# Retrieval layer of an encoder block: six more first-product blocks made ahead, a fourth buffer for finished blocks, and splits that follow the block in front

## The chip, the core and the metric

One core of a Trainium2 chip. The metric is the device time of one execution in microseconds (us). Engines are called PE (matrix products), PEld (its weight loads), DVE (vector), ACT (scalar activations), POOL (GpSimd) and SP (the engine whose queue issues most plain DMAs). In the trace a queue's own entries carry a q (ACTq, SPq).

## The reference, cut to what matters

The program is one whole encoder layer on 1,024 tokens of width 1,024. The change touches only its last part, a retrieval feed-forward layer with 16,384 experts. For every token eight heads choose 16 experts each:

```
s1 = q[..., :half] . keys[0];  s2 = q[..., half:] . keys[1]
top16 of s1, top16 of s2, top16 of their sums  -> expert ids e, scores
g = softmax(scores)
h = gelu(x . peer_u[e])          # first product, 128 numbers per token
x = x + sum_k g*h * peer_v[e]    # second product
```

## The kernel before, in words

The 1,024 tokens are eight tiles of 128. Three tiles (`NG`) are served by **gathers**: for each of 128 choices POOL fetches one row of `peer_u` per token with an indirect DMA (L1154), DVE takes the dot product with the token (L1187), and later the same happens with `peer_v`, where DVE adds the scaled row to an accumulator (L1199). That is 768 fetches, each of 128 rows of 4 KB, and 768 DVE operations.

The other five tiles, 640 tokens, are served **densely**. The experts are 128 blocks of 128. For every block i the first product is h_i = gelu(U_i . x): 48 matmuls of 320 columns, written as four groups of 12 (two token halves, two halves of the contraction). The gates, scattered into a dense array `GD` in DRAM, multiply h_i (L1479, `amake1`), the result is cast to a high part `ah` (ACT, L1481) and a low part `al` (DVE, L1487), and the second product adds it to 640 x 1,024 outputs.

Each weight block is split into a high and a low part. For U_i that is `usplit`: a cast `uh` and a subtraction `ul`; the subtraction runs on POOL (L119), and the cast on POOL in the first of the two phases below and on ACT in the second. For V_i it is `vsplit`: `vh` on ACT, `vl` on POOL.

**The first phase** begins at about 780 us. It makes the gates and, beside them, the first products of some blocks ahead. The order is written by a loop in which each turn has one group of four tokens of gate work (PE `pg` L1100 and three small products L1082 to L1085, ACT copies L1110, every eighth turn a store of `GD`, L1113) and one step of 12 matmuls of a first product (`ustep`, L1236). `K0` = 33 blocks spread over the 128 are made ahead, 31 (`KM`) in this loop and the last two in the passage that follows. Their results go to DRAM (`HDm`). With every turn a credit of planned microseconds is given to a list of DVE and POOL work: the top-16 searches of tiles, and gather steps priced at `GCOST` = 3.0. A turn with a block step gives 3.05, one without gives 2.6. The gather steps of this phase take the dot product with the token in SBUF (`QB`, parts 0 and 1) and write its unused products to part 2 of `QB`.

**The main loop** (L1600 to L1628) has 127 turns. In each the second product of block i goes to four accumulators that stay in PSUM (`accum`, 12 matmuls of 512 columns) and to three of six outputs that take turns in one PSUM bank `prot` (`rotate`, 6 matmuls each); DVE adds the bank to X (L1561) before the next `rotate` may start. Between them stand three places (`ugroup`) where one group of 12 matmuls (L1496) of a first product not made ahead is issued: 95 blocks, 380 groups, 381 places. The gather steps that are left are dealt evenly over the turns. A finished block waits in one of three buffers of 128 x 640 (`hfree`): two of their own and one in parts 0 and 1 of `QB`. Blocks made ahead are loaded back into these buffers (`hload`, L1473). At the head of a turn POOL receives the subtraction of V_{i+1} and, in three turns of four, right behind it the subtraction of the next U (`uahead`).

All queues run in order; PSUM bank `hps` of the first products is single.

Of the kernel before, what the change touches and what calls it, by code (L numbers as in the profile page):

```python
# [10 lines left out]
BF = mybir.dt.bfloat16  # L11
# [3 lines left out]
ALU = mybir.AluOpType  # L15
# [16 lines left out]
NK = 128  # L32
# [7 lines left out]
TB = 32  # L40
GCH = 4
NPERS = 4
K0 = 33
WIN = 2
NVI = 3
NO2 = 2
GPE = 1.4
GCOST = 3.0
KT = 2
GLAST = 1  # L50
FD = 2
# [20 lines left out]
def peer_block(tc, I, out):  # L72
    nc = tc.nc
    ctx = ExitStack()
    V, A, G, PE, SY = nc.vector, nc.scalar, nc.gpsimd, nc.tensor, nc.sync
# [51 lines left out]
    with ExitStack() as fr:  # L127
# [55 lines left out]
        with ExitStack() as st:  # L183
            a_ = st.enter_context(tc.tile_pool(name="A", bufs=1))
            ps = st.enter_context(tc.tile_pool(name="psA", bufs=2, space=PSUM))
# [184 lines left out]
            for j, nm in enumerate(["q_norm_g", "k_norm_g"]):  # L370
                a = I[nm]
# [120 lines left out]
        with ExitStack() as st:  # L492
            b_ = st.enter_context(tc.tile_pool(name="B", bufs=1))
            ps = st.enter_context(tc.tile_pool(name="psB", bufs=1, space=PSUM))
# [270 lines left out]
            for u in range(NU + 4):  # L765
                g = (u + 4) // 4
# [23 lines left out]
                for ch in ORD:  # L790
                    r = parts(ch)
# [33 lines left out]
    TD = ND * P  # L825
    KM = K0 - KT
# [290 lines left out]
    class Gather:  # L1117
# [51 lines left out]
        def adv(self, n=1):  # L1169
            for _ in range(n):  # L1170
                if not self.ready():
                    return
                self.fill()
                ph, t, k = self.seq[self.nc]
                r = self.rows.pop(self.nc)
                self.nc += 1
                ps = self.ps
                if ph == 0:
                    h = self.h(t) if ps is None else ps
                    if k == 0:  # L1180
                        self.hh[t] = gp.tile([P, P], F32, name=f"hh{t}")
                        if ps is not None:
                            self.stage(t)
                            A.copy(ps, self.staged[t])
                            self.slots.append(self.staged.pop(t))
                    jk = QB[:, 2, :].bitcast(BF)
                    V.scalar_tensor_tensor(jk, r, 1.0, h, op0=ALU.mult, op1=ALU.mult,  # L1187
                                           accum_out=self.hh[t][:, k:k + 1])
                else:
                    if k == 0:  # L1190
                        aa = gp.tile([P, P], F32, name=f"aa{t}")
                        A.activation(aa[:], self.hh[t][:], AF.Gelu_apprx_tanh)
                        V.tensor_tensor(aa[:], aa[:], gg[t][:], op=ALU.mult)
                        self.aa[t] = aa
                    xt = X[:, t, :]
                    if k == 0 and ps is not None:
                        A.copy(ps, xt)
                    to = xt if ps is None else ps
                    V.scalar_tensor_tensor(to, r, self.aa[t][:, k:k + 1], to, op0=ALU.mult, op1=ALU.add)  # L1199
                    if k == P - 1 and ps is not None:  # L1200
                        A.copy(xt, ps)
                self.slots.append(r)
                if ph and k == P - 4 and t + 1 < NG and ps is not None:
                    self.stage(t + 1)
# [36 lines left out]
    def gelu_(hps, pool, bufs):  # L1241
        ho = pool.tile([P, TD], F32, name="ho", tag="ho", bufs=bufs)
        A.activation(ho[:].rearrange("p (a b) -> p a b", a=len(segs)), hps[:, :len(segs), :SW], AF.Gelu_apprx_tanh)  # L1243
        return ho
# [40 lines left out]
    def k_gat():  # L1285
        if not ks.get("gat") or not gat.ready():
            return None
        gat.adv(1)
        return GCOST

    def kstep():
        order = [("gen", k_gen), ("topk1", k_topk1), ("gat", k_gat)]
# [49 lines left out]

    ust = dict(i=0, seg=0, hps=None, prev=None)

    def ustep():
        i = ust["i"]
        if i >= KM:
            return 0.0
        if i == 0 and ust["seg"] == 0:
            uload(US[0])  # L1350
            uload(US[1])
            usplit(US[0])
        sg = ust["seg"]
        if sg == 0:
            ust["hps"] = hbank([P, 2, 512], "hps")
        useg(US[i], ust["hps"], 2 * sg, 2 * sg + 2)
        if sg == 1 and ust["prev"] is not None:
            ho = gelu_(ust["prev"], up, 1)
            SY.dma_start(HDm[i - 1], ho[:])
        if sg == 1 and i < KM:  # L1360
            usplit(US[i + 1])
            if i + 2 < K0:
                uload(US[i + 2])
        ust["seg"] += 1
        if ust["seg"] == 4:
            ust["seg"] = 0
            ust["i"] += 1
            ust["prev"] = ust["hps"]
        return 1.65
# [34 lines left out]
    while True:  # L1404
# [4 lines left out]
            break  # L1409
        dt = max(dt + GPE * did, KB)  # L1410
        kadv(dt, dt)
    ho = gelu_(ust["prev"], up, 1)
    SY.dma_start(HDm[KM - 1], ho[:])
    while ks["n2"] < len(korder):
        clk["t"] += 2.0
        kstep()
# [2 lines left out]
    with ExitStack() as vs:  # L1419
# [45 lines left out]
            CH[i] = (vh, vl)  # L1465

        hfree = [vp.tile([P, TD], F32, name=f"ho{j}")[:] for j in range(2)]
        hfree.append(QB[:, 0:2, :].rearrange("p a b -> p (a b)")[:, :TD])

        def hload(i):  # L1470
            if i in UI and i not in HO and i < NK:
# [41 lines left out]


        ulist = [i for i in range(NK) if i not in UI]
        ug = dict(g=0, split=0, load=0, ps=None)

        def uahead():
            m = ug["g"] // 4
            if ug["split"] < min(m + 2, len(ulist)):  # L1520
                usplit(ulist[ug["split"]])
                ug["split"] += 1
                if ug["load"] < len(ulist):
                    uload(ulist[ug["load"]])
                    ug["load"] += 1

        def ugroup():
            m, q = divmod(ug["g"], 4)
            if m >= len(ulist):
                return  # L1530
            i, (hf, d) = ulist[m], divmod(q, 2)
            if ug["split"] <= m:
                uahead()
            if d == 0:
                ug["ps"] = ubank()
            uhalf(i, hf, ug["ps"], d * DC // 2, (d + 1) * DC // 2)
            if d == 1:
                if hf == 0:
                    HO[i] = hfree.pop(0)
                ugelu(HO[i], hf, ug["ps"])  # L1540
            ug["g"] += 1

        def uready(i):
            while i not in UI and ulist.index(i) >= ug["g"] // 4:
# [55 lines left out]
        for i in range(NK - 1):  # L1600
            nx = i + 1
            ng = gat0 + -(-(ngat - gat0) * min(nx, nb) // nb) - gat.nc
            gs = [0] * 3
            for j in range(ng):
                gs[SPOTS[j % len(SPOTS)]] += 1
            hload(nx)
            if len(hfree) > 1:
                hload(i + 2)
            loads(i + 2)
            vsplit(nx)  # L1610
            uahead()
            rs_ = [w for w in range(len(rot)) if i % WIN == w % WIN]
            rotate(rs_[0], i, False)
            accum(i, (0,))
            ugroup()
            gat.adv(gs[0])
            rotate(rs_[1], i, False)
            accum(i, (1,))
            ugroup()
            uready(nx)  # L1620
            amake1(nx)
            gat.adv(gs[1])
            amake2(nx)
            rotate(rs_[2], i, False)
            accum(i, (2, 3))
            ugroup()
            gat.adv(gs[2])
            CH.pop(i - WIN, None)  # L1628
        accum(NK - 1, range(len(pers)))
# [71 lines left out]
```

## Time and profile before

| | |
|---|---|
| median of 3 runs | 2993.06 us (2991.23 to 2999.02) |
| the profiled execution | 2996.14 us, of which the span of instructions is 2994.4 us |
| granted PE clock over the span | 0.979 |
| PE busy | 2799.0 us (93%) |
| DVE busy | 2463.6 us (82%) |
| POOL busy | 1953.6 us (65%) |
| DMA | 710.33 MB, mean 237 GB/s |

Shares of busy time are means over stages that differ. A stage's row gives busy microseconds and number of instructions in the order PE, PEld, DVE, ACT, POOL, then the granted PE clock, the busy share of the DMA engines and GB/s. A line of the timeline gives start, duration, engine, line, operation, output and inputs, and how many were merged; in square brackets stand the idle time just before it and what ended that. Matmuls are pipelined: a matmul's duration is longer than the distance to the next, and the distances between starts tell the pace.

### The profile page before, as it was taken

To read this page: it belongs to the slowest core of one execution; us is meant where nothing else is said; L and a number is where in the kernel's file an instruction comes from. 1 tells how busy PE (TensorE), PEld (TensorE's weight loads), DVE (VectorE), ACT (ScalarE), POOL (GpSimd) and SP (SyncE) were. 2 spreads that over 40 slices of the span, in tenths; PEclk is the share of its full clock that TensorE was granted. 3 is DMA by queue.
4 is the path that set the end of the run, shared out by engine and by line. 5 is a ranking of instruction groups with operands and counts; after the bars stand their busy time and mean duration, and the time that the engine had idled before them with its cause. 6 is when DMAs were issued, how large, how long until landed. Compare 5 with 4: busy or idle time off the path is not lost.

```text
span 2994.4 us, 44528 instructions
## 1 busy us (share of the span) xinstructions
PE 2799.0 (93%) x16042; PEld 2475.3 (83%) x16048; DVE 2463.6 (82%) x4465; ACT 1149.2 (38%) x2376; POOL 1953.6 (65%) x1558
## 2 busy tenths in 40 slices
PE   7878899899989899978999999999999999999997
PEld 6767778698978788867888888888888888888886
DVE  5889988468666967864899988988899999999998
ACT  3216566342577577663222222222222222222222
POOL 2578842104445766764777777777777777777775
PEclk9989999999999999999999999999999999999999
DMA  4111000044334667676899898999999998989996
GB/s 131 46 68 36 8 1 15 33 159 129 106 142 149 219 228 266 211 276 251 330 336 345 332 337 330 349 334 353 335 348 335 349 347 333 341 333 337 341 342 228
DMA packets 296719, 710.33 MB, mean 237 GB/s; under 512 B 25264, under 2 KB 135216, under 8 KB 296368
## 3 DMA queue, kind: packets, MB, share of 16 engines
q0 software_dynamic: 110592, 402.70, 35.2%
q1 hardware_dynamic: 156800, 252.85, 25.1%
q10 hardware_dynamic: 29104, 51.91, 4.6%
q8 instruction: 126, 2.06, 0.3%
q14 instruction: 97, 0.79, 0.1%
HBM read 640.46 MB, written 66.91 MB: 236 GB/s over the span
## 4 chain that ended last, share of the span: by engine, by line
PE 55%; DVE 20%; DMA 8%; issue 7%; POOL 4%; ACT 4%; ACTq 1%; SPq 0%; another core or an unknown queue 0%; POOLq 0%; DVEq 0%
PE hps L1496 15%; PE hps L1236 5%; PE prot L122 5%; PE prot L123 4%; PE prot L124 4%; DVE y L146 3%; PE pg L1100 3%; PE acc L122 3%; PE acc L124 3%; PE acc L123 3%; DMA rows<-peer_v,ei 2%; DMA rows<-peer_u,ei 2%; DVE ga L1199 2%; DVE ho L1479 2%; DVE PT L119 2%
## 5 line engine op out<-in xcount | busy, mean ns | idle before, releaser
L1496 PE MATMUL hps<-HN,uh 128*128 128x320 f32 x3072 | 683.9, 310 | 8.1 <-ACT ho L1243 5.3
L1496 PEld LDWEIGHTS hps<-HN,uh 128*128 128x128 f32 x3072 | 530.4, 189 | 42.4 <-issue 5.5
L1496 PE MATMUL hps<-HN,ul 128*128 128x320 f32 x1536 | 475.6, 310 | 0.0
L1199 DVE SCALAR_TENSOR_TENSOR ga<-rows,aa,ga 128x1024 f32<-128x1024 f32 x330 | 424.0, 1285 | 27.5 <-DMA rows<-peer_v,ei 18.1
L1154 POOL DMA_INDIRECT rows<-peer_u,ei x339 | 360.1, 1062 | 108.0 <-issue 68.7
L119 POOL TENSOR_TENSOR vl<-vr,vh 128x1024 fp32r<-128x1024 f32 x128 | 308.8, 2413 | 156.9 <-ACT vh L116 108.5
L1154 POOL DMA_INDIRECT rows<-peer_v,ei x330 | 326.9, 991 | 112.6 <-issue 72.5
L1187 DVE SCALAR_TENSOR_TENSOR QB<-rows,ga 128x1024 bf16<-128x1024 f32 x271 | 329.7, 1216 | 31.3 <-DMA rows<-peer_u,ei 25.1
L122 PE MATMUL prot<-vh,ah 128*128 128x512 f32 x762 | 309.0, 406 | 27.9 <-DVE X L1561 18.6
L119 POOL TENSOR_TENSOR ul<-ur,uh 128x1024 fp32r<-128x1024 f32 x127 | 324.5, 2555 | 2.6
L1561 DVE TENSOR_TENSOR X<-X,prot 128x512 f32<-128x512 f32 x384 | 262.1, 682 | 65.5 <-PE prot L124 55.2
L123 PE MATMUL prot<-vl,ah 128*128 128x512 f32 x762 | 301.1, 395 | 0.4 <-POOL vl L119 0.4
L124 PE MATMUL prot<-vh,al 128*128 128x512 f32 x762 | 297.5, 390 | 0.0
L1496 PEld LDWEIGHTS hps<-HN,ul 128*128 128x128 f32 x1536 | 289.5, 188 | 0.0
L1506 ACT ACTIVATE ho<-hps 128x320 f32<-128x320 f32 x128 | 55.8, 436 | 493.3 <-PE hps L1496 456.2
L1110 ACT COPY gblk<-pg 128x128 f32<-128x128 f32 x640 | 175.6, 440 | 99.2 <-PE pg L1100 74.2
L116 ACT CAST vh<-vr 128x1024 fp32r<-128x1024 f32 x128 | 133.7, 1045 | 203.3 <-DMA vr<-peer_v 196.0
L1236 PE MATMUL hps<-HN,uh 128*128 128x320 f32 x992 | 210.0, 334 | 0.0
L122 PE MATMUL acc<-vh,ah 128*128 128x512 f32 x512 | 199.6, 390 | 0.0
L124 PE MATMUL acc<-vh,al 128*128 128x512 f32 x512 | 199.6, 390 | 0.0
L123 PE MATMUL acc<-vl,ah 128*128 128x512 f32 x512 | 199.5, 390 | 0.0
L122 PEld LDWEIGHTS prot<-vh,ah 128*128 128x128 f32 x762 | 143.2, 188 | 65.7 <-DVE X L1561 32.6
(273 smaller groups left out, 6550.0 us busy)
## 6 DMA issues: line engine op xcount, KB each, us to landing
ur<-peer_uT SPq DMA_DIRECT2D x128, 512.0 KB
vr<-peer_v SPq DMA_DIRECT2D x128, 512.0 KB
GD<-gblk ACTq DMA_DIRECT2D x80, 512.0 KB
gl<-GD SPq DMA_DIRECT2D x64, 640.0 KB
wqr<-peer_wq SPq DMA_DIRECT2D x32, 512.0 KB
HDm<-ho SPq DMA_DIRECT2D x31, 320.0 KB
s<-SD SPq DMA_DIRECT2D x64, 128.0 KB
ho<-HDm SPq DMA_DIRECT2D x22, 320.0 KB
```

What stands on the lines that cost most here:

```text
L116: A.copy(hi, src)
L119: lo_eng.tensor_tensor(lo, src, f(hi), op=ALU.subtract)
L122: PE.matmul(ps, ah, bh, start=start, stop=False)
L123: PE.matmul(ps, ah, bl, start=False, stop=False)
L124: PE.matmul(ps, al, bh, start=False, stop=stop)
L1110: A.copy(gblk[b][k][:, :, q * 4:q * 4 + 4].rearrange("p i t -> p t i"), pg[:, :, k * w:k * w + w])
L1154: G.indirect_dma_start(out=r, out_offset=None, in_=I["peer_v" if ph else "peer_u"], in_offset=bass.IndirectOffsetOnAxis(ap=ge[t][:, k:k + ...
L1187: V.scalar_tensor_tensor(jk, r, 1.0, h, op0=ALU.mult, op1=ALU.mult, accum_out=self.hh[t][:, k:k + 1])
L1199: V.scalar_tensor_tensor(to, r, self.aa[t][:, k:k + 1], to, op0=ALU.mult, op1=ALU.add)
L1236: PE.matmul(hps[:, j, :b - a], (uh, uh, ul)[st3][:, dc, :], HN[(0, 1, 0)[st3]][:, dc, a:b], start=dc == 0 and st3 == 0, stop=dc == DC - 1 ...
L1496: PE.matmul(ps[:, :b - a], (uh, uh, ul)[st3][:, dc, :], HN[(0, 1, 0)[st3]][:, dc, a:b], start=dc == 0 and st3 == 0, stop=dc == DC - 1 and ...
L1561: V.tensor_tensor(X[:, NG + t, n:n + 512], X[:, NG + t, n:n + 512], pr, op=ALU.add)
```

## The change

- `K0` goes from 33 to 39: 37 blocks in the loop of the first phase, two in the passage, 89 left for the main loop.
- A gather step costs the planner 2.0 instead of 3.0 once the top-16 work of all tiles is done.
- The dot product writes its unused products over the fetched row, in f32, instead of to part 2 of `QB` in bf16. `QB` now gives two buffers for finished blocks, four in all.
- The last block of the first phase is finished (`ulast`) from inside the loop.
- In the main loop a place is filled only when the number of groups is behind an even deal of 356 groups over 381 places, and the first half of a block is finished only if more than one buffer is free.
- The split and the load of the next U are issued right after the first group of the block in front of it, wherever in the turn that is, and no longer at the head of the turn.

```diff
-K0 = 33
+K0 = 39
 GCOST = 3.0
+GCOST2 = 2.0
@@ Gather.adv
-                    jk = QB[:, 2, :].bitcast(BF)
-                    V.scalar_tensor_tensor(jk, r, 1.0, h, op0=ALU.mult, op1=ALU.mult,
+                    V.scalar_tensor_tensor(r, r, 1.0, h, op0=ALU.mult, op1=ALU.mult,
                                            accum_out=self.hh[t][:, k:k + 1])
@@ k_gat
-        return GCOST
+        return GCOST if ks["n2"] < len(korder) else GCOST2
@@
+    def ulast():
+        if ust["prev"] is not None:
+            ho = gelu_(ust["prev"], up, 1)
+            SY.dma_start(HDm[KM - 1], ho[:])
+            ust["prev"] = None
+
     def ustep():
         i = ust["i"]
         if i >= KM:
+            ulast()
             return 0.0
@@
-    ho = gelu_(ust["prev"], up, 1)
-    SY.dma_start(HDm[KM - 1], ho[:])
+    ulast()
@@
-        hfree.append(QB[:, 0:2, :].rearrange("p a b -> p (a b)")[:, :TD])
+        hfree += [QB[:].rearrange("p a b -> p (a b)")[:, j * TD:(j + 1) * TD] for j in range(2)]
@@
-        ug = dict(g=0, split=0, load=0, ps=None)
+        ug = dict(g=0, split=0, load=0, ps=None, slot=1)
@@ ugroup
-            if ug["split"] <= m:
-                uahead()
             if d == 0:
                 ug["ps"] = ubank()
...
             ug["g"] += 1
+            if q == 0:
+                uahead()
+
+        def uslot():
+            ug["slot"] += 1
+            if ug["g"] < -(-4 * len(ulist) * ug["slot"] // (3 * (NK - 1))) and (ug["g"] % 4 != 1 or len(hfree) > 1):
+                ugroup()
@@ main loop
             vsplit(nx)
-            uahead()
             rs_ = [w for w in range(len(rot)) if i % WIN == w % WIN]
             rotate(rs_[0], i, False)
             accum(i, (0,))
-            ugroup()
+            uslot()
             gat.adv(gs[0])
             rotate(rs_[1], i, False)
             accum(i, (1,))
-            ugroup()
+            uslot()
             uready(nx)
             amake1(nx)
             gat.adv(gs[1])
             amake2(nx)
             rotate(rs_[2], i, False)
             accum(i, (2, 3))
-            ugroup()
+            uslot()
             gat.adv(gs[2])
```

## Rows read from the trace of the kernel before

**Rows 1.** Stages: end of the first phase, then the main loop.

```profile
1295.00:1363.00 68.00, 46.52 (x260) 33.28 (x258) 38.61 (x50) 47.94 (x144) 32.74 (x22) 0.89 0.68 250
1381.00:2965.00 1584.00, 1562.21 (x8359) 1380.67 (x8360) 1430.01 (x1778) 389.18 (x549) 1231.87 (x918) 1.00 0.91 337
```

**Rows 2.** Timeline of PE in the main loop: its first matmul, one turn, its end.

```profile
1381.31 0.47 PE L122 MATMUL prot<-vh,ah 128*128 128x512 f32 x1 [1.33 <-issue]
...
2206.98 0.39 PE L122 MATMUL prot<-vh,ah 128*128 128x512 f32 x1
...
2209.04 0.45 PE L1496 MATMUL hps<-HN,uh 128*128 128x320 f32 x2
...
2210.80 0.39 PE L122 MATMUL prot<-vh,ah 128*128 128x512 f32 x1
...
2219.12 0.39 PE L122 MATMUL prot<-vh,ah 128*128 128x512 f32 x1
...
2965.47 0.39 PE L122 MATMUL acc<-vh,ah 128*128 128x512 f32 x1
```

**Rows 3.** The adds of line 1561: durations min/median/max, idle before (us, times).

```profile
L1561 DVE TENSOR_TENSOR X<-X,prot x384: 671/682/689, 1383.3 to 2984.8; 128x512 f32<-128x512 f32 x192
...
  PE prot L124: 55.2, 85
```

**Rows 4.** Gather steps on DVE: two kinds of dot product, and the accumulation.

```profile
L1187 DVE SCALAR_TENSOR_TENSOR QB<-rows,ga x271: 1205/1217/1224, 1383.9 to 2680.7; 128x1024 bf16<-128x1024 f32 x136
...
L1187 DVE SCALAR_TENSOR_TENSOR QB<-rows,QB x68: 1204/1225/3285, 974.2 to 1335.5; 128x1024 bf16<-128x1024 f32 x68
...
L1199 DVE SCALAR_TENSOR_TENSOR ga<-rows,aa,ga x330: 1273/1286/1291, 1521.9 to 2967.6; 128x1024 f32<-128x1024 f32 x165
```

**Rows 5.** The gate product L1479 on DVE: min/median/max; then timeline of DVE and POOL.

```profile
L1479 DVE TENSOR_TENSOR ho<-ho,gl x172: 477/490/3134, 1375.4 to 2963.4; 128x320 f32<-128x320 f32 x172
...
2225.88 3.74 DVE L1479 TENSOR_TENSOR QB<-QB,gl 128x320 f32<-128x320 f32 x2
...
2224.25 2.41 POOL L119 TENSOR_TENSOR vl<-vr,vh 128x1024 fp32r<-128x1024 f32 x1 [2.98 <-ACT vh L116]
2226.61 2.66 POOL L119 TENSOR_TENSOR ul<-ur,uh 128x1024 fp32r<-128x1024 f32 x1
```

**Rows 6.** First products in the first phase, by line: busy, mean ns, idle before.

```profile
L1236 PE MATMUL hps<-HN,uh 128*128 128x320 f32 x992 | 210.0, 334 | 0.0
...
L1236 PE MATMUL hps<-HN,ul 128*128 128x320 f32 x496 | 113.7, 310 | 0.0
```

**Rows 7.** The same view, PE, 1295 to 1363 us: gate products still to do.

```profile
L1100 PE MATMUL pg<-o,o 128*128 128x128 f32 x192 | 29.3, 302 | 5.9 <-ACT gblk L1110 5.5 <-ACT o L1093 0.4
```

**Rows 8.** Timeline of PE: two steps of the first phase, and its end.

```profile
1276.63 0.93 PE L1236 MATMUL hps<-HN,uh 128*128 128x320 f32 x4
...
1279.92 0.93 PE L1236 MATMUL hps<-HN,uh 128*128 128x320 f32 x4
...
1356.74 1.16 PE L1100 MATMUL pg<-o,o 128*128 128x128 f32 x8 [0.37 <-ACT o L1093]
1363.23 0.87 PE L1496 MATMUL hps<-HN,uh 128*128 128x320 f32 x2 [5.33 <-ACT ho L1243]
```

**Rows 9.** Timeline of ACT and its queue: two stores of gates, and the phase's end.

```profile
1210.23 0.33 ACTq L1113 DMA_DIRECT2D GD<-gblk  x1
...
1293.25 0.33 ACTq L1113 DMA_DIRECT2D GD<-gblk  x1
...
1361.13 1.28 ACT L1243 ACT_TABLE_LOAD   x1 [2.19 <-issue]
```

**Rows 10.** Timeline of POOL late in the first phase: a split's cast, top-16, a fetch.

```profile
1281.81 1.04 POOL L118 CAST uh<-ur 128x1024 fp32r<-128x1024 f32 x1 [5.94 <-PE hps L1236]
...
1294.64 2.43 POOL L1020 TENSOR_TENSOR eq<-pf,iota 128x800 f32<-128x800 f32 x1 [0.27 <-DVE e L1028]
1297.23 1.53 POOL L1154 DMA_INDIRECT rows<-peer_u,ei  x1 [0.15 <-issue]
```

## The prediction

> **What bounds the kernel now.** I read the stages first [rows 1]. In the main loop PE is busy 1562 of 1584 us at full granted clock and the DMA share is 0.91; DVE is busy 1430 us. At the end of the first phase no engine is full: PE 46.5 of 68 us, at a granted clock of 0.89. So the loop looks bound by PE and the tail by nothing, and the question is what six blocks cost when they move from the one to the other. Next the pace of PE [rows 2]. A turn without waits lasts 2219.12 - 2206.98 = 12.14 us; a place of 12 matmuls takes 2210.80 - 2209.04 = 1.76 us of it, and nine matmuls of 512 columns take 2209.04 - 2206.98 = 2.06, so three take 0.69. The loop runs from 1381.31 to 2965.47, 1584.2 us for 127 turns. Without waits it would be 127 x 12.14, less the one place that is empty, 1540; some 44 us are PE's waits. Then what DVE waits for [rows 3]: 85 of the 384 adds to X wait for PE, 55 us together. Without these DVE would need 1584 - 55 = 1529 us, its other waits included. The two engines are 11 us apart: the loop is a pair in lockstep, and PE alone cannot be relieved without limit.
>
> **The change, part by part**
>
> *Six blocks fewer in the loop.* The loop loses 24 of 380 places, 24 x 1.76 = 42 us of PE work: 1540 becomes 1498.
>
> *An empty place uncovers the add to X.* Bank `prot` is single. After a `rotate` PE has the accumulators (0.69 us) and a place (1.76 us), together 2.45 us in which DVE must do the add of 0.68 us [rows 3]. With the place empty 0.69 is left after the first or second `rotate`, 1.38 after the third. I walked the new rule for the places through the 127 turns: 24 are left empty, 17 of the first two kinds and 7 of the third, and no block is ever late. The add often starts behind one or two gather steps of 1.2 to 1.3 us [rows 4]; the trace has no `rotate` with so little cover. If DVE is always free, an empty place costs next to nothing; if it never is, the whole 1.76 us is lost, 42 in all. I take 1.0 us for the 17 and 0.5 for the 7, 20 us, because 299 of 384 adds find DVE behind PE.
>
> *Splits that follow the block.* In three turns of four two subtractions stand back to back on POOL at the head of the turn. When V arrives late, both run into DVE's gate product [rows 5]: two products that have a median of 0.49 us each took 3.74 us and ended when POOL's second subtraction did. With the change I count 88 splits in the loop, 30 in the first place of a turn (as before), 29 in the second, just ahead of the gate product, and 29 in the third, behind it. A third gets better, a third can get worse, one turn in four has no split at all. Between nothing and half of PE's 44 us of waits; I take 11 us of gain.
>
> The Trainium skill bears on this, in sentences that the sum does not need. "SBUF — State Buffer", section "SBUF: two separate sides", says that VectorE and GpSimd share a pair of ports that an instruction holds exclusively to its end, and that a VectorE operation with two SBUF inputs takes part. The row agrees: the gate product has two such inputs and ended with the subtraction. By that rule the 29 splits of the second place would cost DVE up to one subtraction, 2.4 us, each, and the sum would come out near -1; by the row's single case and the order of issue I keep a gain.
>
> *The dot's output.* The accumulation, whose output is f32, takes 1.286 us, the dot with a bf16 output 1.217 [rows 4]; but the former writes to PSUM. In place in SBUF I take 1.217, no change; at 1.286 the 307 dots of the loop would cost DVE 21 us, which its distance to PE nearly covers after the change. Writing over the row makes nothing wait: the row's slot was free only after the same dot anyway.
>
> *Fourth buffer, reloads.* Five more blocks come back from DRAM in the loop (128 x 640 f32, 320 KB each) and six U loads (512 KB) leave it; one buffer more lets them come earlier. Cost and gain nothing: the cover is the whole turn in which a reload is ahead. If that cover went, the gate product would be late, then the cast to `ah`, then the next turn's products.
>
> *The tail of the first phase.* 1488 matmuls are 124 steps of 12 [rows 6]; 192 gate products, that is 24 of the 160 groups, are still to do when they end at 1295 [rows 7]. The 24 steps of the six blocks meet exactly these 24 groups. Turns with a step pass at 1279.92 - 1276.63 = 3.29 us [rows 8], and with the waits for gate stores 24 of them took 1293.25 - 1210.23 = 83.0 us [rows 9]. Now the tail takes 68 us [rows 1]. After the last gate product PE waited 1363.23 - 1356.74 = 6.5 us from start to start [rows 8], of which a table load took 1.3 [rows 9] that need not come, since the gelu now runs all along; I take 4. So 83 + 4 - 68 = +19. Lower bound 24 x 3.29 + 4 - 68 = +15. Upper bound from POOL: eight top-16 operations at 2.43, 26 fetches at 1.53 and 0.15, six U casts at 1.04 [rows 10] and six subtractions at 2.66 [rows 5], 19 + 44 + 6 + 16 = 85 us; POOL would be as full as PE, and its lateness could add some 10: +30. The six extra stores of results and six loads of U go to SP's queue ahead of nothing else in this stretch; the DMA share there is 0.68 [rows 1].
>
> *Gather steps.* Walking the credits (3.05 a turn in place of 2.6; price 2.0 in the last 11 turns) gives 77 fetched rows in the first phase where the same walk gives 68 for the kernel before, as the trace has. Nine dots leave the loop, 9 x 1.3 = 12 us of DVE: 1529 becomes 1517. PE does not see this directly.
>
> *The passage to the loop* begins at the lower clock after the idle tail: its first two matmuls lasted 0.87 us against 0.45 for two in the loop [rows 2, 8]. If two dozen run so, an estimate, at twice the loop's 1.76/12 = 0.147 us, they lose 3.5 us. With PE kept busy I take 2 us back.
>
> **Sum.** Loop: -42 + 20 - 11 = -33, which leaves 1551, above both floors of 1498 and 1517. Tail +19, passage -2. Together -16 on the profiled execution's 2996.1, so 2980. Its median of three runs lies 3.1 below; on that basis I predict 2977. A change of 0.3%, 9 us, is about what a measurement tells from nothing.
>
> **Rivals**
>
> *Better (0.15):* late V no longer hits the gate product and empty places are cheap: loop -52, in all -35, 2958. For it: DVE's floor of 1517 allows it. Against: four in five adds find DVE behind PE.
>
> *The transfers set the loop (0.13):* 337 GB/s x 1584 us is 534 MB; nine fetches (0.5 MB each) and the reloads and loads leave 528. At the same rate that is 1566 us, loop -18, in all -1: 2992. For it: share 0.91 [rows 1]. Against: little of DVE's waiting shows on PE.
>
> *The lock (0.14):* the second-place splits cost DVE 29 x 1.7 = 49 us (2.4 less what a product overlaps), nothing is won back: DVE's floor becomes 1566, loop -18, in all -1: 2992.
>
> *Slower (0.14):* DVE sets the pace, and every empty place is lost in the wait for the add to X. Loop 0, tail +19, passage -2: +17, 3010. It decides from the point where an empty place gives back less than 17/24 = 0.7 of its 1.76 us. For it: 299 adds behind PE. Against: 55 us in which DVE waits for PE today.
>
> *Forecast (0.44):* 2965 to 2985.
>
> **Numbers.** Forecast and better lie under 2984: 0.44 + 0.15, less a little for its upper edge, 0.57 faster. Transfers and lock, and that edge, give 0.28 within; 0.15 slower. The low end takes in half of the better case; the upper one the two neutral cases, the tail's bound of +30 (11 above mine) and part of the slower case: 2953 to 3004. The likeliest case alone has 2965 to 2985.
>
> **What would show it.** The first phase's last first product should start near 1378 and the loop near 1398, at a granted clock near 1 throughout; gate stores 27 to 28 us apart. In the loop: a turn of 12.2 us in the mean, `prot` matmuls waiting for X after empty places by about 1 us, gate products with fewer long cases. Wrong would be: stores 31 us apart (POOL or transfers in the tail), adds to X that wait for PE hardly at all (DVE is the pace), or a dot over 1.3 us.

## The result and the profile after

The changed kernel takes 3075.16 us (median of 6 runs, 3066.89 to 3093.37) against 2992.14 us (2989.93 to 2999.02, 6 runs) for the kernel before beside it: a ratio of 1.028 [1.025, 1.031], slower by some 83 us. The forecast was 2977 us with a range to 3004. The profiled execution took 3093.37 us, 97.2 more than that of before.

First the stages of the changed kernel: the end of the first phase, then the main loop from its first matmul to that of the last chunk. They answer to [rows 1].

```profile
1300.00:1380.00 80.00, 75.20 (x522) 68.21 (x521) 58.26 (x65) 49.63 (x142) 66.23 (x42) 1.00 0.81 293
1404.95:3062.86 1657.91, 1555.70 (x8074) 1365.06 (x8074) 1397.36 (x1761) 376.20 (x530) 1207.88 (x903) 0.97 0.88 318
```

The tail is near what was forecast: PE 75.2 of 80 us busy, clock 1.00, and the loop begins at 1404.95, which is 23.6 us later than before (forecast +17). The loop is not: 1657.9 us in place of 1584.2, where 1551 were forecast. The places that are left need 1498 us, so PE lost 160: it sat idle for 1657.91 - 1555.70 = 102 us, and its busy time is 58 us above the 1498. The clock column says why for most of the 58: 0.97 here, 1.00 before.

Next the waits inside the loop (engine and line, tile, what it waited for: us in total, times, longest). The changed kernel, rows of 1420 to 3060 us:

```profile
ACT vh L117 <- DMA vr<-peer_v: 244.6, 36, 13.1
POOL vl L120 <- ACT vh L117: 191.7, 44, 11.9
...
PE prot L123 <- DVE X L1572: 72.7, 48, 6.2
DVE al L1493 <- ACT ah L1487: 56.2, 51, 2.8
...
SPq L1218 <- POOL ul L120: 914.3, 76, 21.3
```

The kernel before, 1420 to 2960 us:

```profile
ACT vh L116 <- DMA vr<-peer_v: 195.6, 30, 7.9
POOL vl L119 <- ACT vh L116: 108.2, 44, 4.9
...
PE prot L122 <- DVE X L1561: 8.7, 25, 1.0
DVE al L1487 <- ACT ah L1481: 12.8, 24, 0.6
...
SPq L1218 <- POOL ul L119: 688.6, 60, 13.8
```

V was late before too: 30 times, 6.5 us each, and each time ACT stood. All 30, and after the change 29 of the 36, are chunks (one in four) whose V is loaded right behind a pair of gate loads. What grew is the length of these waits, from 6.5 to 8.1 us in the mean and from 7.9 to 13.1 us for the longest, and what hangs on them: POOL, then the add to X, then PE. The last row is the other thing to see: on SP's queue the U loads (L1218) wait for POOL's subtraction to free their buffer, for longer and in more turns.

The same stretch of SP's queue in both kernels (a merged line runs from the first issue to the end of the last). Before:

```profile
1592.91 0.33 SPq L1218 DMA_DIRECT2D ur<-peer_uT  x1
1593.33 0.59 SPq L1457 DMA_DIRECT2D vr<-peer_v  x1
1593.97 22.28 SPq L1453 DMA_DIRECT2D gl<-GD  x2
1616.35 0.59 SPq L1457 DMA_DIRECT2D vr<-peer_v  x1
1617.04 0.38 SPq L1218 DMA_DIRECT2D ur<-peer_uT  x1
```

After:

```profile
1578.28 0.44 SPq L1479 DMA_DIRECT2D ho<-HDm  x1
1578.81 0.58 SPq L1463 DMA_DIRECT2D vr<-peer_v  x1
1594.07 0.33 SPq L1218 DMA_DIRECT2D ur<-peer_uT  x1
1594.45 6.38 SPq L1459 DMA_DIRECT2D gl<-GD  x2
1600.87 1.09 SPq L1463 DMA_DIRECT2D vr<-peer_v  x2
```

There are three gate buffers, so the second load of a pair must wait until the gate product of the last chunk of the old pair has been made; V stands behind it. Before, the first load of the pair went out 22 us ahead of the second, and the last of its packets ended 2.7 us before the second went out (2.5 us in the mean of the 31 pairs), so that V had one gate load ahead of it. After, a U load stands in front of the pair and holds it until POOL has subtracted; then both gate loads, 640 KB each, and V leave within 6.4 us: when V goes out at 1600.87, the packets of both gate loads are still under way, those of the first until 1602.8 and those of the second until 1612.7. What becomes of it, in the changed kernel (first ACT, then POOL, then PE):

```profile
1600.86 0.73 ACT L1487 CAST ah<-ho 128x640 fp32r<-128x640 f32 x1 [2.48 <-DVE ho L1485]
1614.66 1.04 ACT L117 CAST vh<-vr 128x1024 fp32r<-128x1024 f32 x1 [13.07 <-DMA vr<-peer_v]
1615.61 0.43 ACT L1512 ACTIVATE ho<-hps 128x320 f32<-128x320 f32 x1
...
1615.78 2.37 POOL L120 TENSOR_TENSOR vl<-vr,vh 128x1024 fp32r<-128x1024 f32 x1 [9.57 <-ACT vh L117]
...
1609.87 0.39 PE L125 MATMUL acc<-vh,al 128*128 128x512 f32 x1
1616.09 0.90 PE L1502 MATMUL hps<-HN,uh 128*128 128x320 f32 x2 [5.83 <-ACT ho L1512]
1616.79 0.47 PE L1502 MATMUL hps<-HN,ul 128*128 128x320 f32 x1
...
1619.46 0.63 PE L123 MATMUL prot<-vh,ah 128*128 128x512 f32 x1
```

V's cast starts 13.8 us after the load's issue. It holds ACT's queue, and in it the gelu that would empty `hps`: PE waits 5.83 us for a gelu that waits for V. POOL waits 9.57 us, and the fetches behind its subtraction with it. The place after the gap takes 1619.46 - 1616.09 = 3.37 us in place of 1.76: the clock has fallen.

### The profile page after: what moved, and what is told of

It reads as the page before. It is cut to its first block, busy times and chain, and to the rows that moved or that the text cites. A ratio compares the mean times of both kernels' runs of the same rounds, so it can differ in the third digit from the quotient of the medians.

```text
span 3091.6 us, 44191 instructions
## 1 busy us (share of the span) xinstructions
PE 2826.9 (91%) x16042; PEld 2498.8 (81%) x16048; DVE 2455.2 (79%) x4465; ACT 1141.5 (37%) x2364; POOL 1968.1 (64%) x1564
## 4 chain that ended last, share of the span: by engine, by line
PE 55%; DVE 18%; DMA 13%; issue 6%; ACT 4%; POOL 2%; ACTq 1%; SPq 0%; POOLq 0%; DVEq 0%
PE hps L1502 13%; DMA vr<-peer_v 6%; PE hps L1236 6%; PE prot L123 4%; PE prot L124 4%; PE prot L125 4%; PE pg L1101 3%; DVE y L147 3%; PE acc L123 2%; PE acc L124 2%; PE acc L125 2%; DMA rows<-peer_u,ei 2%; DMA rows<-peer_v,ei 2%; DVE ga L1199 2%; DVE PT L120 2%
## 5 line engine op out<-in xcount | busy, mean ns | idle before, releaser
L1502 PEld LDWEIGHTS hps<-HN,uh 128*128 128x128 f32 x2880 | 503.8, 191 | 66.0 <-ACT ho L1512 19.6
L1502 PE MATMUL hps<-HN,ul 128*128 128x320 f32 x1440 | 448.6, 312 | 0.0
L1199 DVE SCALAR_TENSOR_TENSOR ga<-rows,aa,ga 128x1024 f32<-128x1024 f32 x329 | 422.5, 1284 | 27.3 <-DMA rows<-peer_v,ei 21.3
L1155 POOL DMA_INDIRECT rows<-peer_u,ei x341 | 366.3, 1074 | 97.2 <-issue 56.0
L1187 DVE SCALAR_TENSOR_TENSOR rows<-rows,ga 128x1024 f32<-128x1024 f32 x264 | 313.6, 1213 | 20.5 <-DMA rows<-peer_u,ei 14.2
L125 PE MATMUL prot<-vh,al 128*128 128x512 f32 x762 | 303.9, 399 | 0.0
L1502 PEld LDWEIGHTS hps<-HN,ul 128*128 128x128 f32 x1440 | 274.4, 191 | 0.0
L1236 PEld LDWEIGHTS hps<-HN,uh 128*128 128x128 f32 x1184 | 193.9, 190 | 21.5 <-issue 0.6
```

Source lines behind the costliest of these rows:

```text
L125: PE.matmul(ps, al, bh, start=False, stop=stop)
L1155: G.indirect_dma_start(out=r, out_offset=None, in_=I["peer_v" if ph else "peer_u"], in_offset=bass.IndirectOffsetOnAxis(ap=ge[t][:, k:k + ...
L1187: V.scalar_tensor_tensor(r, r, 1.0, h, op0=ALU.mult, op1=ALU.mult, accum_out=self.hh[t][:, k:k + 1])
L1236: PE.matmul(hps[:, j, :b - a], (uh, uh, ul)[st3][:, dc, :], HN[(0, 1, 0)[st3]][:, dc, a:b], start=dc == 0 and st3 == 0, stop=dc == DC - 1 ...
L1502: PE.matmul(ps[:, :b - a], (uh, uh, ul)[st3][:, dc, :], HN[(0, 1, 0)[st3]][:, dc, a:b], start=dc == 0 and st3 == 0, stop=dc == DC - 1 and ...
```

## The experiments

The times in the last two columns are medians, the others are read from one profiled execution each; the ratio is to the kernel before on the same chip. *Pair* is the mean distance from the first to the second gate load of a pair on SP's queue, *V* the mean from the issue of the V behind a pair to the start of its cast (both over the 31 pairs of the loop); *loop* is counted as above.

| kernel | pair, us | V, us | loop, us | time, us | ratio |
|---|---|---|---|---|---|
| before | 21.6 | 8.1 | 1584 | 2992 | |
| after | 11.2 | 11.5 | 1658 | 3075 | 1.028 [1.025, 1.031] |
| e1 after, split at head | 14.2 | 10.8 | 1636 | 3077 | 1.027 [1.025, 1.029] |
| e2 before, split follows | 9.4 | 11.0 | 1620 | 3026 | 1.010 [1.007, 1.013] |
| e3 after, V ahead | - | not late | 1558 | 3002 | 1.002 [1.000, 1.003] |
| e4 after, U load last | 21.7 | 9.8 | 1604 | 3028 | 1.010 [1.007, 1.012] |
| e5 e1, three buffers | 14.7 | 11.0 | 1653 | 3075 | 1.027 [1.025, 1.030] |
| e6 before, V ahead | - | not late | 1545 | 2958 | 0.988 [0.986, 0.990] |
| e7 e1, V ahead | - | not late | 1528 | 2966 | 0.991 [0.989, 0.993] |
| e8 before, four buffers | 21.7 | 7.9 | 1579 | 2991 | 1.000 [0.998, 1.002] |
| e9 before, gate pair a turn earlier | 10.9 | 13.6 | 1747 | 3160 | 1.057 [1.054, 1.059] |
| e10 e1, empty places by fours | 21.3 | 8.3 | 1576 | 3010 | 1.005 [1.004, 1.007] |
| e11 e7, U load last | - | not late | 1516 | 2953 | 0.987 [0.985, 0.989] |
| e12 e3, U load last | - | not late | 1534 | 2971 | 0.993 [0.991, 0.996] |
| e13 e9, V ahead | - | not late | 1552 | 2967 | 0.990 [0.988, 0.992] |
| e14 e6, U load last | - | not late | 1546 | 2960 | 0.988 [0.986, 0.990] |

**The split's place (e1, e2).** The first theory was that moving the split, which brings the U load with it, is the whole loss. e1 undoes it, e2 does it alone.

```diff
 e1 (against the changed kernel; e2 is the reverse on the kernel before)
@@ ugroup
+            if ug["split"] <= m:
+                uahead()
...
-            if q == 0:
-                uahead()
@@ main loop
             vsplit(nx)
+            uahead()
```

> Changed kernel with one part undone: the split and load of the next U stand at the head of the turn again; 39 blocks ahead, paced places, four buffers and dots over the row stay. Theory A (the U load waits on SP for a subtraction that now stands late in the turn, and so holds the gate loads and the next V behind it): the two loads of a gate pair are again some 20 us apart instead of 11, V late at most 8 us, the loop falls from 1658 to 1545-1575, the time to 2970-2995. Rival B (empty places uncover the add to X): the loop stays above 1640, the time at 3060-3085. Rival C (the moved subtraction itself, on POOL among the fetches, not the loads): as A, 2970-2995.

> Kernel before with one part done alone: the split and load of the next U follow the first group of the block in front; 33 blocks ahead, every place filled, three buffers. Theory A and rival C: the loop rises from 1584 to 1630-1670, the time to 3040-3080, gate pairs about 11 us apart. Rival B: 2985-3000, no change.

The theory fell. The move alone costs 30 us, but undoing it gives nothing back. In e2 a U load stands between the last V and the pair every time, at 31 pairs out of 31. In e1 this is so at 23 of 31, where the pair is 11.4 us apart and V takes 11.7; at the other eight it is 22.2 and 8.1, as before the change. So the loss goes by the place of the U load, and either part of the change moves it. The time of e1 is the one that rival B gave; e10 and e11 below take B's mechanism away.

**V ahead of the gate loads (e3, e6).**

```diff
 loads (e3 on the changed kernel, e6 on the kernel before)
+                vload(i)
                 if i % GCH == 0:
                     gload(i)
-                vload(i)
```

> Changed kernel with the load of V issued ahead of the two gate loads of the same turn instead of behind them. Theory A: V is no longer held by the gate pair, late V falls from 244 us in all to under 60, the loop to 1540-1590, the time to 2960-3005. Rivals B and C: V comes earlier, but the loop stays above 1630, the time at 3050-3085.

> The kernel before with one edit: a chunk's V load is issued ahead of its two gate loads. Theory A (the in-order wait of V behind the gate pair already costs the kernel before, through ACT, POOL and the add to X): the waits for V in the chunks with a gate pair go, 196 us on ACT, and PE gets back a half or more of its 46 us of waits: loop 1555 to 1570, 2967 to 2985 us. Rival (at 8 us late it is covered, and only lateness beyond that costs): 2990 to 3000 us.

e3 gives back 74 of the 83 us and its loop, 1558 us, is near the forecast's 1551, though by terms that offset one another (see the part on the prediction). e6 shows that the kernel before pays too. Its loop, in the columns of [rows 1], has almost no wait of PE left:

```profile
1384.08:2928.70 1544.62, 1541.00 (x8361) 1381.92 (x8362) 1324.80 (x1778) 385.47 (x548) 1237.39 (x918) 1.00 0.92 346
```

1544.6 us against a floor of 1540: some 40 of the 44 us of waits that PE had before hung on V's place behind the gate loads.

**The U load behind the next turn's loads (e4).**

```diff
@@ uahead
-                if ug["load"] < len(ulist):
-                    uload(ulist[ug["load"]])
-                    ug["load"] += 1
+                ug["due"] = True
+        def ulate():
+            if ug.pop("due", False) and ug["load"] < len(ulist):
+                uload(ulist[ug["load"]])
+                ug["load"] += 1
@@ main loop
             loads(i + 2)
+            ulate()
```

> Changed kernel with only the place of the U load on SP's queue moved: the split stays where the change put it, its load of the block after next is issued behind the next turn's gate and V loads. Theory A: SP no longer waits for the subtraction ahead of the gate pair, pairs 18-22 us apart, the loop 1555-1600, the time 2980-3020 (a U that comes late may cost some of it). Rival B and rival C: the loop stays above 1630, the time 3050-3085.

The pair is 21.7 us apart again, and 48 us come back, over half. V is still late in the chunks with a pair, 31 times by 6.4 us, and PE still waits 60 us for the add to X (72.7 after).

**The fourth buffer (e5, e8).** One buffer more lets reloads out earlier, ahead of gates and V.

```diff
 e5 (against e1)
-        hfree += [QB[:].rearrange("p a b -> p (a b)")[:, j * TD:(j + 1) * TD] for j in range(2)]
+        hfree += [QB[:].rearrange("p a b -> p (a b)")[:, j * TD:(j + 1) * TD] for j in range(1)]
 e8 (against the kernel before)
-                    V.scalar_tensor_tensor(jk, r, 1.0, h, op0=ALU.mult, op1=ALU.mult,
+                    V.scalar_tensor_tensor(r, r, 1.0, h, op0=ALU.mult, op1=ALU.mult,
@@
-        hfree.append(QB[:, 0:2, :].rearrange("p a b -> p (a b)")[:, :TD])
+        hfree += [QB[:].rearrange("p a b -> p (a b)")[:, j * TD:(j + 1) * TD] for j in range(2)]
```

> The changed kernel with the subtraction and its U load back at the head of the turn (as e1) and, in addition, with three buffers for finished blocks in place of four (the six blocks ahead, the rule for the places and the dots in place stay). Theory F (the fourth buffer, by sending reloads from DRAM earlier ahead of the gate loads and of V on SP's queue, is the other part of the loss that e1 left): V in the chunks with a gate pair is late by about 8 us as before the change, loop 1555 to 1590, 2985 to 3015 us. Rival P (the six blocks ahead themselves: the empty places take away PE's cover, the buffer does not matter): stays at 3060 to 3090 us with V late by 10 us and more.

> The kernel before with one part of the change: the fourth buffer for finished blocks, with the dots' products written over the fetched row (33 blocks ahead, split at the head, a block at every place). Theory F (earlier reloads on SP's queue make V later): the two gate loads come closer together than 21.6 us, V is late by 10 us and more, loop 1600 to 1640, 3010 to 3050 us. Rival P (the buffer costs nothing): 2990 to 3000 us. A dearer dot would add 15 to 20 us with V unchanged.

This theory fell on both sides: without the buffer e1 is as slow, and with it, the dots in place included, the kernel before is as fast as ever.

**Both orders (e7).** e1 and e3 together.

```diff
 against e1
+                vload(i)
                 if i % GCH == 0:
                     gload(i)
-                vload(i)
```

> The changed kernel with the split at the head of the turn (e1) and the V load ahead of the gate loads (e3) together. Theory A (only V's place behind the gate pair made the change slow): as e3 or a little off it, 2990 to 3010 us, whichever place the split has; gate products dearer than in e3 by the two subtractions that stand together. Rival (the split's move has a price of its own, apart from V): under e3 by 15 to 30 us, 2970 to 2985 us.

The rival's number came: with V out of the way the split's place has still some 30 us. Some 13 us of that go through the U load in front of the gate loads, the rest does not (e11 and e12 below).

**The phase (e9, e10).** What e1, e2 and the change have in common is when a U load stands ahead of a gate pair. In the kernel before a block is four groups and a turn has three places, so three blocks take four turns exactly, and a pair of gate loads comes every four turns. Counted from the order of issue, splits and U loads come in turns 0, 2 and 3 of four (31 each) and in turn 1 never; the pair is issued in turn 2. So the free turn always lies just ahead of the pair. With the split behind the first group the free turn is turn 3; with 24 empty places strewn evenly it wanders (e1: 20, 23, 20 and 24 splits in the four turns). e9 moves the pair and nothing else; e10 keeps e1's 24 empty places but leaves four in a row empty, six times, which puts every block back into its phase (29, 0, 29, 29).

```diff
 e9 (against the kernel before)
+        def gbase(i):
+            return 0 if i < 3 else min((i - 3) // GCH * GCH + 3, NK - GCH)
@@ amake1
-                V.tensor_tensor(o, o, gl[i - i % GCH, hf][:, :, i % GCH, :], op=ALU.mult)
+                V.tensor_tensor(o, o, gl[gbase(i), hf][:, :, i - gbase(i), :], op=ALU.mult)
@@ loads
-                if i % GCH == 0:
-                    gload(i)
+                if i == 0 or i % GCH == 3:
+                    gload(gbase(i))
 e10 (against e1)
-            if ug["g"] < -(-4 * len(ulist) * ug["slot"] // (3 * (NK - 1))) and (ug["g"] % 4 != 1 or len(hfree) > 1):
+            left = min(24, 4 * ((24 * (ug["slot"] - 2) + 300) // (4 * 3 * (NK - 1))))
+            if ug["slot"] - 2 - ug["g"] >= left and (ug["g"] % 4 != 1 or len(hfree) > 1):
```

> The kernel before with one edit: the groups of four chunks that share a pair of gate loads begin at chunks 3, 7, 11, ... in place of 4, 8, 12, ..., so that the pair is issued one turn earlier in the pattern of four turns (one pair of loads more in all; nothing else moves). In the kernel before three blocks take exactly four turns, and the one turn in four that issues no U load is the one just ahead of the gate pair. Theory G (what matters is whether a U load that waits for POOL stands on SP's queue in the turn ahead of the gate pair): now one always does, so the two gate loads come 9 to 12 us apart in place of 21.6, V behind them is late by 10 us and more, as in e2: 3010 to 3035 us. Rival (the phase is irrelevant, it is the split's place or the empty places as such): 2985 to 3000 us.

> e1 (the changed kernel with the split at the head of the turn) with the same 24 empty places, but left empty four in a row, six times, so that each block keeps its place in the pattern of four turns and no U load stands in the turn ahead of a gate pair. Theory G: V is late by about 8 us as before the change, gate loads 21 to 24 us apart, loop 1550 to 1580, 2980 to 3010 us. Rival P (empty places take away PE's cover, wherever they stand): four in a row uncover at least as many adds to X, so 3050 to 3090 us.

Both went the way of the phase. e10 is 67 us faster than e1 with the same work and the same number of empty places; its pairs are 21.3 us apart. e9 is 166 us slower than the kernel before, much more than expected. Its SP queue, and POOL behind it:

```profile
1603.88 0.33 SPq L1218 DMA_DIRECT2D ur<-peer_uT  x1
1604.26 10.54 SPq L1456 DMA_DIRECT2D gl<-GD  x2
1614.84 1.84 SPq L1460 DMA_DIRECT2D vr<-peer_v  x2
...
1629.62 2.38 POOL L119 TENSOR_TENSOR vl<-vr,vh 128x1024 fp32r<-128x1024 f32 x1 [8.10 <-ACT vh L116]
1631.95 2.93 POOL L119 TENSOR_TENSOR ul<-ur,uh 128x1024 fp32r<-128x1024 f32 x1
```

Here V is late in turn 2, whose third place begins the very block that is split at the turn's head, behind V's split on POOL; so the first product waits as well (before, V is late in turn 3, and the block that is split there begins a turn later):

```profile
POOL vl L119 <- ACT vh L116: 240.1, 29, 10.7
...
PE hps L1499 <- POOL ul L119: 86.1, 27, 3.5
```

That row is absent from the waits of before.

**Whether V is all of it (e13), and the orders with the U load last (e11, e12, e14).**

```diff
 e13 (against e9; e11 to e14 have the same order of V and gates)
+                vload(i)
                 if i == 0 or i % GCH == 3:
                     gload(gbase(i))
-                vload(i)
 e11 (against e7), e12 (against e3), e14 (against e6): the U load as in e4
             loads(i + 2)
+            ulate()
```

> e9 (the kernel before with the gate pair one turn earlier in the pattern, 3160 us) with V ahead of the gate loads, as in e6 (2958 us). Theory G (the phase costs only through V, which stands behind the gate pair): no late V, no POOL that waits 240 us for ACT, 2955 to 2985 us, the upper part if the gate loads, now behind the U load, make the gate product wait. Rival (the U load in the turn ahead costs by itself, through gate loads and the subtractions of U): 3010 us or more.

> e3 (the changed kernel with V ahead of the gate loads, the split still following the block) with the U load issued behind the next turn's V and gate loads. e3 is some 30 us slower than e7, which has the split at the head. Theory Q (the split's move costs by the place of the U load on SP's queue): the U load no longer stands ahead of gate loads, 2955 to 2975 us. Rival (it costs by the subtraction's place on POOL, in front of the gather's fetches and of V's subtraction): 2985 to 3005 us.

> e7 (the changed kernel, split at the head, V ahead of the gate loads) with the U load issued behind the next turn's V and gate loads. Theory Q (what is left in e7 is gate loads that come late behind a waiting U load): DVE's wait for the gate loads falls from 31 us to under 15, loop 1505 to 1525, 2945 to 2962 us. Rival (the waits for gate loads come from their own buffers, or U comes too late now): 2962 to 2985 us.

> e6 (the kernel before with V ahead of the gate loads, 2958 us) with the U load issued behind the next turn's V and gate loads. In e6 PE's waits in the loop are 7 us in all, so that nothing on SP's queue has more than that to give: 2950 to 2960 us, as e6. With the six blocks ahead in addition this is e11 (2953 us), whose loop is 28 us shorter and whose first phase is 19 us longer. Rival (a U load that is issued one turn later comes too late for a block at every place): 2965 us or more.

e13 takes back some 193 us of e9's time with the phase left wrong: the phase costs through V. Between e13 and e6 lie 6 to 9 us, by the ratios and by the medians, which is all that the U load in front of the gates can have cost by itself there. In the changed kernel the same move is worth more: 26 to 31 us come back from e3 to e12, where the split follows the block, and 13 from e7 to e11, where it stands at the head. The 18 us between e12 and e11 belong to the split's place itself, with U and V out of the way; what they go through is taken up under "The lock" below. e11 is the fastest, 2953 us, and its loop is the cleanest that the 89 blocks had:

```profile
1403.38:2919.72 1516.34, 1507.74 (x8073) 1338.90 (x8074) 1321.01 (x1761) 376.28 (x530) 1205.72 (x903) 1.00 0.94 348
```

e14 and e6, without the six blocks, lie at 0.988 [0.986, 0.990], e11 at 0.987 [0.985, 0.989]: the gain over the kernel before is the order of the loads; what the six blocks add to it is too little to be told.

## Why the prediction was wrong

**The step that failed** is "Splits that follow the block". It priced the moved split on POOL and DVE alone, -11 us, and left out the DMA that the split issues: the U load, with its wait for POOL, on SP's in-order queue, where gates and V stand behind it. The step "An empty place uncovers the add to X" has the same hole: an empty place also moves every later U load by a third of a turn against the gate pair. I had read the late V [rows 5] only as the reason why subtractions meet the gate product, and not asked what sets its lateness, nor how near that was to being worse. Even with V and U out of the way the moved split did not gain the 11 us: from e11 to e12 it costs 18.

**The size.** Against the same kernel with V ahead and U last, the loop of before lost 1584 - 1546 = 38 us (e14), that of after 1658 - 1534 = 124 (e12). The difference, 86 us, is what the change added through V and the loads around it. The loop's +74 is then the sum of three: -30 for six blocks fewer with 24 places empty (e14 to e11), +18 for the split's place (e11 to e12) and +86. These are profiled executions, and that of the changed kernel lies 18 us above its median, so the 86 may be that much too large. The forecast had -42 + 20 - 11 = -33. The two parts do not add up: split alone +36 on the loop (e2), the 24 strewn places with the split at the head +60 over the same places in phase (e1, e10), both together no more than 22 over the latter alone (after, e1).

**Two other terms held, where V is not in the way.** From e14 to e11 the loop loses 1546 - 1516 = 30 us; -42 + 20 = -22 were forecast, so 24 empty places cost some 12 us and not 20, if the other edits between the two cost nothing. The loop starts 1403.4 - 1382.6 = 21 us later, +17 forecast. With V late, places that are empty cost more: e10, with its pairs and its V much as before, has a loop only 8 us shorter than before in place of 30, and its PE waits 35.4 us for the add to X against 8.7. That a late V and an empty place meet at that add is argued, not shown.

**The tail and the passage.** The passage's first matmul starts 1383.35 - 1363.23 = 20 us later than before, +19 forecast for the tail; the last first product of the tail starts at 1381.2 for 1378. Two distances between gate stores are 27.4 us, as forecast; the last one is 33.1, and ACT waits 2.79 us in it for an earlier store to land. From the passage's first matmul to the loop's it took 1404.95 - 1383.35 = 21.6 us, 18.1 before: +3.5 where -2 was forecast, and PE was not kept busy there as I had it (8 of 15 us from 1390 on, clock 0.91). Rows of ACT's queue, of ACT and, last, of PE:

```profile
1294.73 0.33 ACTq L1114 DMA_DIRECT2D GD<-gblk  x1
...
1322.16 0.33 ACTq L1114 DMA_DIRECT2D GD<-gblk  x1
...
1349.59 0.33 ACTq L1114 DMA_DIRECT2D GD<-gblk  x1
...
1361.79 1.28 ACT L1111 COPY gblk<-pg 128x128 f32<-128x128 f32 x5 [2.79 <-DMA GD<-gblk]
...
1382.64 0.33 ACTq L1114 DMA_DIRECT2D GD<-gblk  x1
...
1383.35 0.53 PE L1502 MATMUL hps<-HN,uh 128*128 128x320 f32 x2 [1.79 <-ACT gblk L1111]
```

**Dots and buffers at nothing: right.** The dot in place takes what it took [rows 4], and e8 puts both edits at 1.000. The count of 77 rows fetched early held too. The dots (min/median/max):

```profile
L1187 DVE SCALAR_TENSOR_TENSOR rows<-rows,ga x264: 1204/1214/1223, 1407.6 to 2767.2; 128x1024 f32<-128x1024 f32 x132
L1187 DVE SCALAR_TENSOR_TENSOR rows<-rows,QB x77: 1206/1225/3406, 977.7 to 1371.9; 128x1024 f32<-128x1024 f32 x77
```

**The lock: not on the gate product, but one row further.** The subtraction that makes `al` is also a product of DVE with two inputs in SBUF, and it comes behind the gate product. After the change 31 of its 127 run beside a subtraction of U, 20 of them beside one of the 29 splits of the second place; before none did. The two by line in the loop (busy us, mean ns, idle before), first before:

```profile
L1479 DVE TENSOR_TENSOR ho<-ho,gl 128x320 f32<-128x320 f32 x170 | 175.3, 1070 | 3.7 <-DMA ho<-HDm 1.9 <-ACT ho L1506 1.8
L1479 DVE TENSOR_TENSOR QB<-QB,gl 128x320 f32<-128x320 f32 x84 | 81.8, 1013 | 0.0
L1487 DVE TENSOR_TENSOR al<-ho,ah 128x640 fp32r<-128x640 f32 x85 | 70.0, 824 | 8.6 <-ACT ah L1481 8.5
...
L1487 DVE TENSOR_TENSOR al<-QB,ah 128x640 fp32r<-128x640 f32 x42 | 34.7, 827 | 4.9 <-ACT ah L1481 4.9
```

After:

```profile
L1493 DVE TENSOR_TENSOR al<-QB,ah 128x640 fp32r<-128x640 f32 x63 | 100.6, 1597 | 37.9 <-ACT ah L1487 37.9
L1485 DVE TENSOR_TENSOR QB<-QB,gl 128x320 f32<-128x320 f32 x126 | 92.7, 770 | 22.1 <-DMA gl<-GD 22.1
L1485 DVE TENSOR_TENSOR ho<-ho,gl 128x320 f32<-128x320 f32 x128 | 82.3, 683 | 2.7 <-DMA ho<-HDm 2.7
...
L1493 DVE TENSOR_TENSOR al<-ho,ah 128x640 fp32r<-128x640 f32 x64 | 68.1, 1064 | 18.6 <-ACT ah L1487 18.3
```

The 254 gate products fall from 257 to 175 us, the 127 of `al` rise from 105 to 169. In e2, the move alone, it is -45 and +53. So the gain that I gave this step is not there even on DVE. With V and U out of the way (e11 to e12) both rise, by 11 and by 20 us, and the loop is 18 us longer; the rival had 49 us on DVE. That these 31 us of DVE are the way in which the split's place costs PE 18 is argued; its place ahead of the fetches on POOL is not separated from it.

**DVE's floor** was none. I had taken 1584 - 55 = 1529 us, 1517 after the change, for the least that DVE needs. With V ahead (e6) the same instructions keep DVE busy for 1324.8 us in place of 1430.0, 118 us less of it in the gate products, and the loop of e11, 1516 us, lies under the floor.

**The rival on the other side** had the sign and the wrong mechanism: empty places were to be lost in the wait for the add to X. PE's waits for that add did grow, from 8.7 to 72.7 us, but with V ahead of the gates and U last (e11, rows of 1420 to 2920 us) they are 7.0 with the same number of empty places:

```profile
PE prot L123 <- DVE X L1575: 7.0, 15, 1.0
```

**The rival of the transfers** fell too: 337 GB/s was to be the most that the loop moves, and e11 moves 348.

## What to carry to other kernels

An instruction that is moved takes its DMAs along, and meets other neighbours: write down, for each in-order queue, which wait it carries and what stands behind it, before pricing the engines; and price every operation that it can now run beside, not only the one that it leaves. Where two patterns with a common period share a queue, look at their phase; skipping a step now and then is enough to lose a good one. And a load that another engine's queue hangs on belongs ahead of loads that wait for a buffer: here that alone was worth 1.2% of the kernel before.

## What the runs showed of the hardware

A gap of PE costs more than its length. Stretches of 20 us of the changed kernel around the late V above, in the columns of the stages:

```profile
1580.00:1600.00 20.00, 20.00 (x111) 18.00 (x110) 18.09 (x21) 4.76 (x7) 14.76 (x11) 1.00 0.85 296
1600.00:1620.00 20.00, 14.17 (x68) 12.51 (x67) 12.98 (x15) 3.67 (x5) 8.59 (x9) 0.85 0.75 278
```

After 5.83 us without a matmul the next 12 took 3.37 us in place of 1.76, about the lower level, 1.2 of 2.4 GHz; the granted clock of the stretch is 0.85. Over the loop the same number of matmuls (8074 and 8073 records) kept PE busy for 1555.7 us after, at a granted clock of 0.97, and 1507.7 in e11, at 1.00: some 48 of the 142 us between the two loops are clock.

How long a load of 512 KB is on its way depends on what was issued just ahead of it: from its issue to V's cast 8.1 us pass in the mean behind one gate load that has landed and one that has not, 13.8 us in the case above behind two that have not. The Trainium skill ("DMA: Bandwidth & Descriptors", section "Queues, rings and completion order") says that the loads of one issuing engine share one ring on each DMA engine, whose descriptors are consumed in order. The runs fit that: V issued ahead of the pair is never late in the chunk with a pair (e3, e6). But there V also no longer stands behind SP's wait for a gate buffer, and no run separates the two.

A product of DVE with two inputs in SBUF that meets a subtraction of POOL is stretched. After the change `al` takes 2.5 us in the mean where a subtraction of U runs beside it (31 of 127) and 0.82 where none does; before, none of the 127 met one, and they took 0.81 to 0.88.
